# A hybrid-attention layer on one core: squares of the norms in two f32r parts, another booked clock, another plan, and the first low parts on VectorE

## The chip, the core and the metric

The kernel runs on one core of a Trainium2 chip. The metric is the device time of one execution in microseconds (us); a version's time is the median of several runs.

## What is computed

One layer on 528 tokens (16 meta tokens and 512 of the sequence) of width 1024, all in float32. The mixer has three kinds of attention with their own projections out of one matrix w_in: stick-breaking (sb, 4 heads), index-selected sparse attention (sp, 4 heads, the 132 best keys of each query by an index score), and differential attention (df, 4 heads, each the difference of two softmaxes). A gated sum of the three goes through w_out, then follows a convolutional gated feed-forward part. What the change touches are the norms of the heads:

```python
def _rmsnorm(a, gain):
    af = a.astype(jnp.float32)
    af = af * lax.rsqrt(jnp.mean(af * af, axis=-1, keepdims=True) + EPS)
    return (af * gain.astype(jnp.float32)).astype(a.dtype)
...
    q_df = _rmsnorm(q_df.reshape(b, tp, DF_HEADS, 2, HEAD_DIM), q_norm_df)
    k_df = _rmsnorm(k_df.reshape(b, tp, DF_HEADS, 2, HEAD_DIM), k_norm_df)
...
    y_df = _rmsnorm(y_df, subln_df) * (1.0 - lam_init)
```

q and k of sp are normed in the same way (over 64 elements); the output of df over 128.

## The kernel before, in words

**Precision.** A float32 product is made of three f32r products: every weight chunk (128 x 1024) and every activation is split into a high part (rounded to f32r by ScalarE) and a low part (the rest, by a subtraction), and mm3 (L336) runs high x high, high x low and low x high into one bank. A chunk used by the projections costs 48 matmuls, 24 for each half of the tokens.

**Chunks.** The 133 weight chunks are used in a fixed order (list order, made from the plan). prep (L315) loads one on SP's queue, rounds it on ScalarE and subtracts on VectorE or, through sub (L108), on VectorE or GpSimd, whichever the booked clock says is done first, VectorE with a handicap of 1000 ns. From the eleventh chunk on every second one (set two, L296) takes another way: two DMAs on GpSimd's queue with a negated copy on ScalarE between, so that no engine subtracts.

**The order of the work.** PLAN (L46) lists the stages. sb0, df2, sp1 and the like are units of two heads (df: one head of double width): q, k and v are projected by three chunks, and then generators take over: q_stream and k_stream (L665, L683) norm, split and move q and k by DMAs on SP's queue into the layout of the scores; v_stream (L701) transposes v; weight_stream (L880) makes the attention weights, one unit after another (after_unit, L1002), for sp only when the selection of the keys (topk_stream, L590) is done; value_stream (L893) multiplies by v; y_stream (L986) norms (df only) and splits the output. g0a and the like are four gate chunks each. b0a and the like are the branch products of one kind; branch (L1050) waits by until (L233) for the outputs of all units of its kind: b0 needs sb0 and sb1, b2 needs df0 to df3, b1 needs sp0 and sp1.

**The booked clock.** The program text is laid out by a planner in Python: mm, V, S and G add a cost to a clock of their engine (book, L77; Timed, L83; pe, L124), and each generator has a time at which its last result should be there (the engine's clock plus LAT). tick (L195), called after every eight matmuls, lets every generator go on; settle (L222) holds one back until TensorE's clock is past its results, ease (L228) until VectorE's clock is not far ahead of TensorE's. So the booked costs decide how early or late side work is put between the projections' matmuls. The queues themselves are in order, and buffers are counted: 13 tmp tiles, 12 qk tiles (a unit takes 6), 2 v, 8 y, 8 banks.

**headnorm** (L639) is the norm of q, k and the df outputs. It takes four tmp tiles: squares (ScalarE), then for each half of the tokens one float32 matmul with a constant matrix (blk: blocks of -0.5/64; ones2: -0.5/128) that sums over the head, then rstd (L428: logarithm, exponential and square on ScalarE) and rstd2 (L435: two operations on VectorE), at the end one multiplication on VectorE. It is called 16 times: for q and k of the two sp and four df units, and for the four df outputs. In the profile all matmuls are on L183, all operations of ScalarE, VectorE and GpSimd on L99.

Of the kernel before, what the change touches and what calls it, by code (L numbers as in the profile page):

```python
# [8 lines left out]
F32 = mybir.dt.float32  # L9
F32R = mybir.dt.float32r  # L10
AF = mybir.ActivationFunctionType
OP = mybir.AluOpType
# [3 lines left out]
P = 128  # L16
# [26 lines left out]

PLAN = "sb0 sb1 g0a df0 df1 g2a g0b df2 b0a b0b df3 g2b sp0 sp1 b2a b2b g1a g1b b1a b1b"  # L46
UNITS = {"sb": 0, "sp": 2, "df": 4}
BRW, BRO = (2, 2, 4), (0, 2, 4)

# [1 line left out]
def nk(i):  # L51
    return NM + P * (i + 1)
# [3 lines left out]
def tile_kernel(ctx: ExitStack, tc, hT, wpk, par, bias, yT):  # L56
    nc = tc.nc
# [5 lines left out]

    clock = {"P": 0.0, "V": 0.0, "S": 0.0, "G": 0.0}
    main = {"t": 0.0}
    cur = [main]
    LAT = 150.0
    SLACK = 1800
    BSL = 500
    PACE = 13000  # L70
# [6 lines left out]
    def book(e, cost):  # L77
        c = cur[0]
        clock[e] = max(clock[e], clock["P"]) + cost
        c["t"] = max(clock[e], c["t"] + cost, clock["P"] + cost) + LAT  # L80

    class Timed:
# [11 lines left out]
        def __getattr__(self, op):  # L94
            f = getattr(self.eng, op)

            def run(out, *a, **k):
# [2 lines left out]

            return run

    V = Timed("V", nc.vector, 1.04, 150, scalar_tensor_tensor=(1.25, 105), tensor_tensor_scan=(2.16, 110),
              tensor_tensor_reduce=(1.0, 255), match_replace=(1.04, 220))
    S = Timed("S", nc.scalar, 0.84, 190)
    G = Timed("G", nc.gpsimd, 2.3, 200)

    def sub(out, a, b, hv=HV):  # L108

# [14 lines left out]
    def pe(cost):  # L124
        c = cur[0]
        ready = c["t"] if c["t"] != c.get("pe") and c is not main else 0
        clock["P"] = max(clock["P"], ready) + cost
        c["t"] = c["pe"] = clock["P"] + LAT


    const = ctx.enter_context(tc.tile_pool(name="const", bufs=1))
# [44 lines left out]
    def tmp(dt=F32):  # L176
        return ap_.tile([P, T], dt, tag="tmp", bufs=caps["tmp"], name="tmp")

    def mm(out, lhsT, rhs, **k):

        n, w = rhs.shape[-1], 0.84 * max(32, lhsT.shape[-1])
        pe(max(0.46 * n + 1, w) if rhs.dtype == F32R else 2 * max(0.844 * n, w))
        PE.matmul(out, lhsT, rhs, **k)  # L183
# [38 lines left out]
    def settle(more=0):  # L222

        c = cur[0]
        while clock["P"] < c["t"] + more + SLACK:
            yield
# [23 lines left out]
    make_identity(nc, ident)  # L250
    onesd = const.tile([P, P], F32, name="onesd")
    V.memset(onesd, -0.5 / D)
    ones2 = const.tile([P, P], F32, name="ones2")
    V.memset(ones2, -0.5 / 128)
    blk = const.tile([P, P], F32, name="blk")
    V.memset(blk, 0.0)
    V.memset(blk[0:64, 0:64], -0.5 / 64)
    V.memset(blk[64:128, 64:128], -0.5 / 64)
    eps = const.tile([P, 1], F32, name="eps")
    V.memset(eps, EPS)  # L260
    one = const.tile([P, 1], F32, name="one")
# [15 lines left out]
    wraw, wsp = {}, {}  # L277
    plan = PLAN.split()
    order = [W_IX, W_QIX, W_QIX + 1]
    for w in plan:  # L280
# [5 lines left out]
        else:  # L286
            n = BRW[br] // 2
# [8 lines left out]
    two = set(order[10:order.index(W_OUT):2])  # L296
# [18 lines left out]
    def prep(k):  # L315
        if k is None or k in wsp:
            return
        assert k not in two
        load(k)
        r = wraw[k]  # L320
        wh, wl = parts_of(k)
        S.copy(wh, r)
        a = after.get(k)
        if a in two:
            V.tensor_tensor(wl, r, wh, OP.subtract)
        else:
            sub(wl, r, wh, HVW)
        load(a)
        if a in two:
            wh, wl = parts_of(a)  # L330
            gdma(wh, chunk(a))
            S.activation(wl, wh, AF.Copy, scale=-1.0)
            book("G", 1050)
            nc.gpsimd.dma_start(wl, chunk(a), accum_op=OP.add)  # L334
# [76 lines left out]
    ixd, st = [wbank(), wbank()], [wbank(), wbank()]  # L411
# [27 lines left out]
    y0, a0 = tmp(), tmp()  # L439
# [150 lines left out]
    def topk_stream():  # L590
        cur[0]["t"] += TKS
        yield from settle()
        for i in range(NB):
            c0 = 2 + P * i
            V.memset(work[i][:, nk(i):], -2e38)
            for j in range(8):
                for o, n in pieces(i):
                    yield from wait("tmp")
                    yield from ease(2000)
                    st, b = yield from bank("w")  # L600
                    cur[0]["t"] = 0
                    mm(st[:, :n], qst[j // 4][:, j % 4, c0:c0 + P], kst[:, o:o + n], start=True, stop=True)
                    r = tmp()
                    S.activation(r[:, :n], st[:, :n], AF.Relu)
                    drop(b)
                    x = r[:, :n]
                    acc = cmask[:, 384 - P * i + o:384 - P * i + o + n] if j == 0 else work[i][:, o:o + n]
                    if i == 0:
                        x = rev(x)
                        acc = acc if j else rev(acc)  # L610
                    V.scalar_tensor_tensor(work[i][:, o:o + n], x, wcol[:, i, j:j + 1], acc,
                                           OP.mult, OP.subtract if i == 0 and j == 0 else OP.add)
                    give("tmp")
        give("y")
        for r in range(-(-TOPK // 8)):
            t0 = clock["P"]
            for i in range(NB):
                left = count[i] - 8 * r
                if left <= 0:
                    continue  # L620
                yield from ease(500)
                m8 = ap_.tile([P, 8], F32, tag="m8", bufs=8, name="m8")
                book("V", 1.04 * nk(i) + 140)

                tc.keep_in_program_order(V.max(m8, work[i]))
                if left < 8:
                    V.memset(m8[:, left:], -2e38)
                V.match_replace(work[i], m8, work[i], -3e38)
                yield
            while clock["P"] < t0 + PACE:  # L630
                yield

        V.tensor_scalar(negs[0], rev(work[0][:, :nk(0)]), -3e38, NEG, OP.is_equal, OP.mult)
        for n in negs[1:]:
            V.tensor_scalar(n, n, -3e38, NEG, OP.not_equal, OP.mult)
        picked.append(1)


    def headnorm(raw, n, gain, mat):  # L639

        yield from wait("tmp", 4)
        sq, r, y0, a = tmp(), tmp(), tmp(), tmp()
        S.activation(sq[:, :n], raw[:, :n], AF.Square)
        yield from settle()
        for o, w in (HALQ if n == TQ else HALF):
            t0 = cur[0]["t"]
            st, b = yield from bank("w")
            cur[0]["t"] = 0
            mm(st[:, :w], mat, sq[:, o:o + w], start=True, stop=True)
            x = r[:, o:o + w], st[:, :w], y0[:, o:o + w], a[:, o:o + w]  # L650
            rstd(*x, now=False)
            yield from settle(-SET)
            rstd2(*x)
            drop(b)
            yield
        V.scalar_tensor_tensor(raw[:, :n], raw[:, :n], gain, r[:, :n], OP.mult, OP.mult)
        give("tmp", 4)
# [449 lines left out]
    for m in range(8):  # L1107
        nc.sync.dma_start(hm[:, m], hT[:, m, Q0:])
        k = W_OUT + m
# [19 lines left out]
        sq = ss if m == 0 else ft()  # L1129
# [36 lines left out]
    for f in range(NF):  # L1166
# [11 lines left out]
        a = ft()  # L1178
# [9 lines left out]
    for m in range(8):  # L1188
# [3 lines left out]
        for c in sorted({e // 8 for e in range(e0, e1)}):  # L1192
            k = W_DN + c
# [4 lines left out]
                start=es[0] == e0, stop=es[-1] == e1 - 1)  # L1198
# [77 lines left out]
```

## Time and profile before

| | us |
|---|---|
| median of 3 runs | 896.43 (896.34 to 900.48) |
| profiled execution | 900.03 |
| its span, first to last instruction | 898.2 |

| engine | busy us | share of the span |
|---|---|---|
| TensorE (PE) | 870.2 | 97% |
| VectorE (DVE) | 536.1 | 60% |
| ScalarE (ACT) | 454.6 | 51% |
| GpSimd (POOL) | 248.9 | 28% |

A row of a group of instructions reads: line, engine, operation, tile written <- tiles read, shape, x count | busy us, mean ns of one | idle time before them <- who ended it. A row of the timeline begins with start and duration in us; instructions of one group that follow each other are merged (x8), and the idle time of the engine before them stands in brackets with the releaser. A row of windows gives for a stretch the busy time of each engine, with the number of instructions begun, and PEclk, the granted share of TensorE's clock. A float32 matmul leaves two records in the trace, an f32r one a single record. The mixer's part ends near 474 us; then follow w_out and the feed-forward part.

### The profile page before, as it was taken

The page shows a single profiled execution, that of the slowest core. Times are in us where ns is not written, and L with a number is a line of the kernel's source. Part 1 is how long each engine was busy: PE and PEld are TensorE (multiplying, and loading weights), DVE is VectorE, ACT ScalarE, POOL GpSimd, SP SyncE. Part 2 cuts the span into 40 slices and gives each one's busy share as a digit, 9 for nine tenths or more (in the row PEclk, how much of TensorE's full clock was granted, in tenths as well). Part 3 has the DMA queues.
Part 4 walks back from the last instruction along what each step waited for, and adds up shares of the span by engine and source line. Part 5 has one row for each costly group of instructions (what it writes and reads, how often), then busy time and mean ns, then how long its engine had stood idle before and what let it go on. Part 6 is the DMA issues. An engine that isn't in the chain of part 4 may idle for free.

```text
span 898.2 us, 15407 instructions
## 1 busy us (share of the span) xinstructions
PE 870.2 (97%) x6066; PEld 807.8 (90%) x6066; DVE 536.1 (60%) x1145; ACT 454.6 (51%) x848; POOL 248.9 (28%) x200
## 2 busy tenths in 40 slices
PE   7899999999999999799999999999999999999998
PEld 6888999999998999699999999999999999888886
DVE  7669969888887787686457544444454544322221
ACT  7457887787756687645553443333333333211110
POOL 2334012122112111664034234444444444200100
PEclk9999999999999999899999999999999999999999
DMA  6666635574547645544454323233333322333330
GB/s 235 163 177 210 163 86 124 133 168 111 121 109 156 164 105 137 120 125 92 121 118 164 96 94 94 94 94 94 95 93 95 92 88 92 103 117 106 118 104 27
DMA packets 35959, 107.79 MB, mean 120 GB/s; under 512 B 4713, under 2 KB 4857, under 8 KB 35888
## 3 DMA queue, kind: packets, MB, share of 16 engines
q1 hardware_dynamic: 27968, 78.19, 28.7%
q0 software_dynamic: 7920, 28.64, 14.9%
q8 instruction: 47, 0.77, 0.4%
q14 instruction: 24, 0.20, 0.1%
HBM read 93.99 MB, written 5.86 MB: 111 GB/s over the span
## 4 chain that ended last, share of the span: by engine, by line
PE 72%; DVE 9%; ACT 7%; DMA 6%; issue 5%; POOL 1%; SPq 1%; ACTq 0%; POOLq 0%; DVEq 0%
PE psd L183 50%; PE psw L183 21%; DVE tmp L99 4%; ACT tmp L99 3%; DMA wl<-wpk 2%; DMA qk<-qk 2%; PE psw L187 2%; DVE work L99 1%; DMA wr<-wpk 1%; DVE wl L99 1%; DMA wh<-wpk 1%; DVE m L99 1%; ACT wl L99 1%; ACT G L99 1%; ACT wh L99 1%
## 5 line engine op out<-in xcount | busy, mean ns | idle before, releaser
L99 ACT CAST wh<-wr 128x1024 fp32r<-128x1024 f32 (+2 forms) x112 | 114.1, 1021 | 201.6 <-DMA wr<-wpk 168.5
L99 DVE TENSOR_TENSOR wl<-wr,wh 128x1024 fp32r<-128x1024 f32 (+2 forms) x80 | 96.2, 1203 | 71.6 <-PE psd L183 67.9
L99 POOL TENSOR_TENSOR wl<-wr,wh 128x1024 fp32r<-128x1024 f32 x32 | 81.5, 2548 | 176.6 <-PE psd L183 95.0
L183 PE MATMUL psd<-xh,wh 128*128 128x258 f32 (+2 forms) x792 | 118.9, 289 | 4.0 <-DVE tmp L99 3.5
L183 PE MATMUL psd<-xl,wh 128*128 128x258 f32 (+2 forms) x792 | 118.2, 289 | 0.0
L183 PE MATMUL psd<-xh,wl 128*128 128x258 f32 (+2 forms) x792 | 116.7, 288 | 1.2 <-POOL wl L99 1.1
L183 PEld LDWEIGHTS psd<-xh,wh 128*128 128x128 f32 x792 | 104.7, 190 | 5.7 <-issue 3.6
L183 PEld LDWEIGHTS psd<-xh,wl 128*128 128x128 f32 x792 | 104.1, 190 | 2.4 <-POOL wl L99 1.3
L183 PEld LDWEIGHTS psd<-xl,wh 128*128 128x128 f32 x792 | 104.4, 191 | 0.5
L99 ACT ACTIVATE tmp<-tmp 128x528 f32<-128x528 f32 (+7 forms) x154 | 69.6, 475 | 17.2 <-DVE tmp L99 14.6
L99 POOL TENSOR_TENSOR ft<-ft 128x512 f32<-128x512 f32 x22 | 47.1, 2140 | 83.5 <-DVE ft L99 83.5
L99 DVE SCALAR_TENSOR_TENSOR ft<-ft,prm 128x512 f32<-128x512 f32 x44 | 48.0, 1090 | 30.1 <-ACT ft L99 29.3
L334 POOL DMA_DIRECT2D wl<-wpk x25 | 22.2, 888 | 130.1 <-ACT wl L99 105.6
L183 PE MATMUL psw<-uh,wh 128*128 128x256 f32 (+2 forms) x264 | 47.0, 320 | 0.0
L183 PE MATMUL psd<-ul,wh 128*128 128x258 f32 (+2 forms) x264 | 46.9, 319 | 0.0
L183 PE MATMUL psw<-ul,wh 128*128 128x256 f32 (+2 forms) x264 | 46.9, 319 | 0.0
L183 PE MATMUL psd<-uh,wl 128*128 128x258 f32 (+2 forms) x264 | 46.8, 319 | 0.0
L183 PE MATMUL psw<-uh,wl 128*128 128x256 f32 (+2 forms) x264 | 46.8, 319 | 0.0
L183 PE MATMUL psd<-uh,wh 128*128 128x258 f32 (+2 forms) x264 | 46.8, 319 | 0.0
L183 PE MATMUL psd<-al,wh 128*128 128x512 f32 x176 | 45.8, 396 | 0.0
L183 PE MATMUL psd<-ah,wl 128*128 128x512 f32 x176 | 45.8, 396 | 0.0
L183 PE MATMUL psd<-ah,wh 128*128 128x512 f32 x176 | 45.8, 396 | 0.0
(196 smaller groups left out, 1674.7 us busy)
## 6 DMA issues: line engine op xcount, KB each, us to landing
wr<-wpk SPq DMA_DIRECT2D x106, 512.0 KB, 3.6
wh<-wpk POOLq DMA_DIRECT2D x25, 512.0 KB, 3.9
wl<-wpk POOLq DMA_DIRECT2D x25, 512.0 KB, 5.6
qk<-qk SPq DMA_DIRECT2D x48, 132.0 KB, 2.5
gd<-tab SPq DMA_DIRECT2D x8, 328.0 KB, 5.5
tmp<-hT SPq DMA_DIRECT2D x8, 264.0 KB, 6.2
W<-gd POOLq DMA_DIRECT2D x8, 264.0 KB, 3.9
qk<-tmp SPq DMA_DIRECT2D x16, 128.5 KB, 4.4
```

The costliest lines, as they stand in the source:

```text
L99: return f(out, *a, **k)
L183: PE.matmul(out, lhsT, rhs, **k)
L187: PE.transpose(out, x, ident[:x.shape[0], :x.shape[0]])
L334: nc.gpsimd.dma_start(wl, chunk(a), accum_op=OP.add)
```

## The change

The norms' squares are written twice by ScalarE, once in float32 and once rounded to f32r, VectorE makes their difference, and two f32r matmuls take the place of a float32 one; blk and ones2 become f32r (their values are exact in it), and the later tiles r and a reuse the squares' tile. The low part of a chunk among the first eleven goes to VectorE whatever the clock says. In the plan df2 and g0b change places, and sp0 and g2b. The booked costs of VectorE, ScalarE and GpSimd lose 60 to 100 ns of fixed cost each, and LAT, the time from the end of an operation to the next engine's start, rises from 150 to 250 ns.

```diff
-PLAN = "sb0 sb1 g0a df0 df1 g2a g0b df2 b0a b0b df3 g2b sp0 sp1 b2a b2b g1a g1b b1a b1b"
+PLAN = "sb0 sb1 g0a df0 df1 g2a df2 g0b b0a b0b df3 sp0 g2b sp1 b2a b2b g1a g1b b1a b1b"
...
-    LAT = 150.0
+    LAT = 250.0
...
-    V = Timed("V", nc.vector, 1.04, 150, scalar_tensor_tensor=(1.25, 105), tensor_tensor_scan=(2.16, 110),
-              tensor_tensor_reduce=(1.0, 255), match_replace=(1.04, 220))
-    S = Timed("S", nc.scalar, 0.84, 190)
-    G = Timed("G", nc.gpsimd, 2.3, 200)
+    V = Timed("V", nc.vector, 1.04, 70, scalar_tensor_tensor=(1.25, 30), tensor_tensor_scan=(2.16, 40),
+              tensor_tensor_reduce=(1.0, 180), match_replace=(1.04, 140))
+    S = Timed("S", nc.scalar, 0.84, 90)
+    G = Timed("G", nc.gpsimd, 2.3, 140)
...
-    ones2 = const.tile([P, P], F32, name="ones2")
-    V.memset(ones2, -0.5 / 128)
+    ones2 = const.tile([P, P], F32R, name="ones2")
+    V.memset(ones2.bitcast(F32), -0.5 / 128)
...
         a = after.get(k)
-        if a in two:
+        if a in two or k in order[:11]:
             V.tensor_tensor(wl, r, wh, OP.subtract)
         else:
             sub(wl, r, wh, HVW)
...
-                book("V", 1.04 * nk(i) + 140)
+                book("V", 1.04 * nk(i))
...
         yield from wait("tmp", 4)
-        sq, r, y0, a = tmp(), tmp(), tmp(), tmp()
+        sq, sh, sl, y0 = tmp(), tmp(F32R), tmp(F32R), tmp()
         S.activation(sq[:, :n], raw[:, :n], AF.Square)
+        S.activation(sh[:, :n], raw[:, :n], AF.Square)
+        V.tensor_tensor(sl[:, :n], sq[:, :n], sh[:, :n], OP.subtract)
+        r, a = sq, sq
         yield from settle()
         for o, w in (HALQ if n == TQ else HALF):
             t0 = cur[0]["t"]
             st, b = yield from bank("w")
             cur[0]["t"] = 0
-            mm(st[:, :w], mat, sq[:, o:o + w], start=True, stop=True)
+            mm(st[:, :w], mat, sh[:, o:o + w], start=True, stop=False)
+            mm(st[:, :w], mat, sl[:, o:o + w], start=False, stop=True)
```

blk is changed as ones2 is.

## Rows read from the trace of the kernel before

**Rows 1.** The page, busy us (share of the span) and instructions of two engines.

```profile
PE 870.2 (97%) x6066; PEld 807.8 (90%) x6066; DVE 536.1 (60%) x1145; ACT 454.6 (51%) x848; POOL 248.9 (28%) x200
```

**Rows 2.** Windows: two stretches of the mixer, then the feed-forward part.

```profile
60.00:80.00 20.00, 17.30 (x137) 16.32 (x136) 19.97 (x46) 14.47 (x40) 12.43 (x7) 1.00 0.54 175
...
360.00:380.00 20.00, 14.50 (x82) 12.36 (x82) 12.67 (x42) 12.91 (x35) 11.83 (x12) 0.83 0.57 125
...
480.00:890.00 410.00, 410.00 (x2437) 362.31 (x2436) 173.46 (x218) 131.39 (x161) 114.32 (x53) 1.00 0.32 101
```

**Rows 3.** Windows: the stretches with a granted clock of 0.50.

```profile
32.50:35.90 3.40, 3.40 (x17) 3.17 (x16) 1.57 (x5) 0.83 (x3) 0.00 (x0) 0.50 0.81 292
...
281.70:285.10 3.40, 3.40 (x19) 3.31 (x18) 0.84 (x8) 1.66 (x8) 1.36 (x2) 0.50 0.95 220
...
370.40:377.20 6.80, 6.57 (x30) 6.02 (x28) 5.64 (x24) 3.42 (x12) 5.14 (x5) 0.50 0.24 56
```

**Rows 4.** Groups of the norms' matmuls, then the timeline of TensorE near 357 us.

```profile
L183 PE MATMUL psw<-tmp,blk 128*128 128x264 f32 (+2 forms) x48 | 14.6, 390 | 0.3 <-ACT tmp L99 0.2
L183 PE MATMUL psw<-tmp,ones 128*128 128x258 f32 (+1 forms) x16 | 4.8, 383 | 0.0
...
356.58 0.59 PE L183 MATMUL psw<-tmp,blk 128*128 128x256 f32 x2
...
357.99 1.14 PE L183 MATMUL psd<-xl,wh 128*128 128x264 f32 x8
...
358.97 1.13 PE L183 MATMUL psd<-xh,wl 128*128 128x264 f32 x8
```

**Rows 5.** Groups by form on ScalarE and VectorE, and one row of the timeline.

```profile
L99 ACT ACTIVATE tmp<-tmp 128x514 f32<-128x514 f32 x10 | 6.3, 627 | 0.0
L99 DVE TENSOR_TENSOR tmp<-tmp 128x528 f32<-128x528 f32 x11 | 9.7, 881 | 0.2
...
15.48 0.70 DVE L99 TENSOR_TENSOR tmp<-tmp 128x528 f32<-128x528 f32 x1
```

**Rows 6.** The timeline: low parts on GpSimd and what stands beside them.

```profile
20.44 4.76 POOL L99 TENSOR_TENSOR wl<-wr,wh 128x1024 fp32r<-128x1024 f32 x2 [15.83 <-DVE tmp L99]
...
27.81 2.35 POOL L99 TENSOR_TENSOR wl<-wr,wh 128x1024 fp32r<-128x1024 f32 x1 [2.60 <-PE psw L183]
...
28.32 2.12 DVE L99 TENSOR_TENSOR kst<-tmp 32x264 fp32r<-32x264 f32 x1
...
30.93 0.42 DVE L99 TENSOR_TENSOR kst<-tmp 32x264 fp32r<-32x264 f32 x1
...
31.05 1.20 PE L183 MATMUL psd<-xh,wh 128*128 128x258 f32 x8 [3.47 <-DVE tmp L99]
...
71.36 5.32 POOL L99 TENSOR_TENSOR wl<-wr,wh 128x1024 fp32r<-128x1024 f32 x1 [4.21 <-issue]
...
76.74 1.26 PE L183 MATMUL psd<-xh,wl 128*128 128x264 f32 x8 [1.10 <-POOL wl L99]
...
258.60 1.22 DVE L99 TENSOR_TENSOR wl<-wr,wh 128x1024 fp32r<-128x1024 f32 x1
```

**Rows 7.** The timeline: df2's q norm, and its first scores.

```profile
243.11 0.60 PE L183 MATMUL psw<-tmp,blk 128*128 128x258 f32 x2
...
260.62 0.65 PE L183 MATMUL psw<-tmp,blk 128*128 128x256 f32 x2
...
281.38 0.48 PE L183 MATMUL psw<-qk 128*2 128x16 f32 x3 [1.93 <-DMA qk<-qk]
```

**Rows 8.** The timeline: b2a's first products, and df3's output.

```profile
360.18 1.08 PE L183 MATMUL psd<-y,wh 128*128 128x258 f32 x6
...
370.96 0.62 ACT L99 CAST y<-tmp 128x514 fp32r<-128x514 f32 x1 [0.27 <-DVE tmp L99]
```

More of the change, by code (lines that the diff above doesn't have):

```diff
@@ L252, in tile_kernel @@
     V.memset(onesd, -0.5 / D)
-    ones2 = const.tile([P, P], F32, name="ones2")
-    V.memset(ones2, -0.5 / 128)
[L255 to L258, printed above, removed]
+    ones2 = const.tile([P, P], F32R, name="ones2")
+    V.memset(ones2.bitcast(F32), -0.5 / 128)
+    blk = const.tile([P, P], F32R, name="blk")
+    V.memset(blk.bitcast(F32), 0.0)
+    V.memset(blk.bitcast(F32)[0:64, 0:64], -0.5 / 64)
+    V.memset(blk.bitcast(F32)[64:128, 64:128], -0.5 / 64)
     eps = const.tile([P, 1], F32, name="eps")
```

## The prediction

> **What bounds the kernel now.** I read the page's busy times first, then the windows, then the timeline around the idle places of TensorE. TensorE is busy 870.2 us of the 898.2 us span and VectorE 536.1 us [rows 1], so the end is set by TensorE's queue: time is won where TensorE gets less work or waits less. From 480 us on (w_out's tail, the feed-forward part) TensorE is busy all of 410 us at the full clock [rows 2]; the diff touches nothing there. The change is decided in the first 480 us, where TensorE has holes. The reader is to see in the windows that two are deep: 60 to 80 us has 17.30 us of TensorE beside a VectorE that is busy 19.97 of 20, and 360 to 380 us has 14.50 [rows 2]. The third group shows what a hole costs behind itself: after each of the waits near 28, 280 and 366 us the granted clock is 0.50 (1.2 of the two levels 1.2 and 2.4 GHz) for 3.4, 3.4 and 6.8 us [rows 3]. At half the clock half of such a stretch is lost: 1.7, 1.7 and 3.4 us.
>
> **Part 1, the squares' products in f32r.** headnorm's matmul runs in float32 today: 48 records with blk and 16 with ones2, two for each matmul, so 32 matmuls (16 norms, two halves each) [rows 4]. One of them with the eight projections behind it lasts from 356.58 to 357.99, 1.41 us; the next eight alone 0.98 us, to 358.97 [rows 4]. So it takes 1.41 - 0.98 = 0.43 us of the queue. It becomes two f32r matmuls of the same width, which at 0.98 / 8 take 0.245 us. The record count stays as it is, 64. Gain 32 x 0.185 = **5.9 us**, all of it on TensorE's queue.
>
> Each norm gets a second Square on ScalarE, 0.63 us [rows 5], 10.1 us in all, and a subtraction on VectorE. The nearest rows for that: 0.70 us undisturbed, 0.88 us as the mean of eleven 528-column forms, some of which collided with GpSimd [rows 5]. I take 0.70, the same operation and operands when nothing else runs: 16 x 0.70 = 11.2 us, at most 14.1. Both lie beside projections' matmuls, which do not wait for a norm. But the norm's product now waits for VectorE as well as for ScalarE, and TensorE's queue is in order: what stands behind it are projections, scores and transposes, and settle's booked time is all that keeps it from being issued too early. The cover ends where a norm is late, as df3's output norm is in front of b2a. There 0.63 + 0.70 = 1.3 us is added to the wait. Together with a few waits at queue heads I put **+2 us** for it, between 0 (all covered) and +5 (a third of the 14.1 us uncovered). No buffer is added: r and a now overwrite the squares.
>
> **Part 2, the first chunks' low parts.** Chunks 3 to 9 of the order have their low part on GpSimd: seven subtractions, the first in the pair at 20.44 us, the last at 71.36 us [rows 6]. The rule k in order[:11] puts all seven on VectorE, 1.22 us each [rows 6], 8.5 us more for it. What goes: the row at 28.32 shows kst's subtraction taking 2.12 us while GpSimd's low part ran from 27.81 to 30.16; its twin at 30.93 took 0.42 [rows 6]. TensorE waited 3.47 us for an evacuation queued behind it (31.05 us) and 1.10 us at 76.74 us for a low part that needed 5.32 us on GpSimd [rows 6]. Against that, a low part of 1.22 us can now stand in VectorE's queue ahead of that same evacuation, and behind it the next operations of the stick-breaking and index scores. At 28 us I book 1.70 - 1.22 = 0.5 us won, at 76 us the 1.10 us, and half a microsecond for the rest: **-2 us**. Bounds: -6 (both waits and the half-clock stretch at 32.5 us gone) and +3 (two and a half low parts added where VectorE is full, at 60 to 80 us).
>
> The skill bears on this. The row shows a two-input VectorE subtraction that lasted until GpSimd's ended. The Trainium skill, page "SBUF — State Buffer", section "Who interferes with whom", says that a VectorE instruction with two SBUF inputs and a GpSimd instruction that reads SBUF lock each other out for the whole instruction. That speaks for part 2, but against part 1: the 16 new subtractions have that form. If every one met GpSimd as kst did, they would cost 16 x 1.70 = 27 us of VectorE on top; by that the last rival below would be likelier, while the sum by the rows stands.
>
> **Part 3, the plan.** df2 moves ahead of g0b, sp0 ahead of g2b; no instruction is added. Today df2's q norm has its first product at 243.11 us and its second at 260.62 us [rows 7]: b0a and b0b ran between, whose evacuations fill VectorE. Its scores then stop TensorE for 1.93 us at 281.38 us, for the DMA that moves q and k [rows 7], and the half clock follows. With four gate chunks behind df2 its norms run before b0a. I take the 1.9 + 1.7 us as won, less a little: **-3.5 us** (0 to -3.6). The larger hole is b2a: its first six products run at 360.18 us, and df3's output is rounded for them only at 370.96 us [rows 8]. That hole is 20 - 14.50 = 5.5 us idle plus 3.4 us of half clock, 8.9 us. df2's weights and values out of df3's way bring df3 forward, but df3 keeps its distance to b2a, and sp0's two norms now follow it directly in place of a gate. I take half, **-4.5 us**; bounds -8.9 (gone) and +8.9 (as long again).
>
> SP's queue gets the same moves of q and k in another order; GpSimd's queue loses seven subtractions, and the chunk loads it issues for every second chunk stay.
>
> **Part 4, the booked clock.** It issues nothing. Lower fixed costs and a larger latency change where ease and settle release work. The trace of before has no row for that; the nearest are the waits of 1 to 2 us above, of one or two more or fewer: **0**, between -3 and +4.
>
> **Sum.** -5.9 + 2 - 2 - 3.5 - 4.5 + 0 = -13.9 us. The profiled execution took 900.03 us (span 898.2 and 1.8 around it): 886.1. It stands 3.6 us above the median of 896.43, so the forecast for the median is 896.4 - 13.9 = **882.5 us**.
>
> **The rivals.** *The hole at b2a stays.* df3's place relative to b2a is unchanged, so its output may come just as late: then -9.4 us, 887. For it: the sum of the work between them is the same; against it: df2's late norm, which now goes ahead. Chance 0.20.
> *All holes close.* -5.9 - 5.5 - 3.6 - 8.9 = -24, 872.5 us. The lower booked cost of VectorE would have to release the norms early everywhere. Chance 0.07.
> *sp0's norms delay df3 (slower).* Its place is between df3 and b2a. Headnorm takes four of 13 tmp buffers, as do df3's weights; if df3's k norm, weights or output norm are held once as df2's q norm is today, 260.62 - 243.11 = 17.5 us, b2a's hole grows by that: -9.4 + 17.5 = +8, 904.5. It decides from the point at which df3's output comes over 9.4 us later relative to b2a's first product than the 10.8 us of today. Against it: g2b's chunks now lie behind sp0 and give time. Chance 0.13.
> *VectorE sets the pace.* 8.5 us of low parts and 11 to 14 us of subtractions, or more with collisions, go to an engine that is full at 60 to 80 us [rows 2]; TensorE's saved 5.9 us and the closed waits come back as waits for evacuations. -13.9 + 14 = 0, 896. Against it: 12.67 of 20 at the large hole [rows 2]. Chance 0.15.
>
> **How the numbers follow.** A measurement here can tell about 0.5% (4.5 us) from no change. The forecast, 878 to 888, has 0.45; the first two rivals, 0.27, are faster as well: faster 0.72, same 0.15 (VectorE), slower 0.13 (sp0). The range leaves out the slower rival and the lower end of the closed holes: 872 to 898, which also holds the bounds of the parts unless most of them fall to one side.
>
> **What would show it.** Right: blk and ones2 products at a pitch of an ordinary f32r matmul; 16 more VectorE and ScalarE operations on tmp; no low part on GpSimd before 100 us and kst at 0.42 us; df2's scores without a DMA wait and the clock at full behind them; TensorE over 16 of 20 us around b2a's start. Wrong: a new TensorE wait of several microseconds with a half clock behind it, above all at b2a or at the first use of sp0's or sp1's q and k; or VectorE over 19 of 20 us in window after window from 100 to 340 us.

## The result and the profile after

The changed kernel took 905.71 us (median of four runs, 903.97 to 909.14), the kernel before 896.38 us beside it: a ratio of 1.0103, 95% interval 1.0065 to 1.0142. It is slower by 1%, where 882.5 us was forecast. The profiled execution took 907.28 us, its span is 905.5 us. In after TensorE's matmuls are on L184 and its transposes on L188 (L183 and L187 before); L99 is as before.

The page of after, busy times of the engines:

```profile
PE 871.6 (96%) x6066; PEld 809.1 (89%) x6066; DVE 549.0 (61%) x1171; ACT 459.2 (51%) x864; POOL 227.5 (25%) x190
```

VectorE has 26 instructions and 12.9 us more than in [rows 1], GpSimd 21.4 us less, TensorE as many records as before. Of the 26, 16 are the new subtractions and seven the low parts; the other three come from the planner, which also picks by its booked clock whether VectorE or GpSimd makes the low part of q, k and the outputs. So the parts were built as described; the 7.3 us that the span grew is not work that was added to TensorE.

A trace shows one execution, and the executions of a version differ with the granted clock (of the changed kernel's four, 903.97 us had 0.992 over the whole span and the profiled one 0.985; e1's trace below is of its longest execution, 907.34 us, f1's of one near its shortest, 893.50 us), so a time read from a single trace can be some microseconds off, while a place in a queue is the same in each.

Windows of after (start:end and length, then busy us and instructions of PE, PEld, DVE, ACT, POOL, then the granted clock, DMA share, GB/s):

```profile
20.00:40.00 20.00, 20.00 (x161) 19.43 (x160) 12.86 (x32) 11.21 (x25) 1.49 (x1) 1.00 0.55 148
60.00:80.00 20.00, 15.56 (x125) 14.61 (x123) 17.76 (x45) 11.72 (x31) 3.87 (x3) 0.98 0.75 214
360.00:380.00 20.00, 17.06 (x117) 14.84 (x117) 17.16 (x42) 14.52 (x36) 7.32 (x7) 0.90 0.44 113
400.00:420.00 20.00, 16.43 (x137) 15.77 (x135) 13.70 (x35) 5.98 (x17) 13.58 (x14) 1.00 0.53 127
```

The reader is to see three things. At 20 to 40 us TensorE never stops. At 60 to 80 us it stops longer than in [rows 2], with a VectorE that is less full. At 360 to 380 us it is busier than in [rows 2], with 4.5 us more of VectorE, and a new hole stands at 400 to 420 us, where the window of before was full:

```profile
400.00:420.00 20.00, 20.00 (x170) 19.75 (x170) 14.64 (x54) 10.39 (x26) 9.76 (x10) 1.00 0.41 107
```

Windows of after, the stretches with a granted clock of 0.50 (0.51):

```profile
79.20:82.60 3.40, 3.07 (x14) 3.06 (x15) 1.38 (x6) 3.40 (x13) 0.93 (x1) 0.51 0.99 252
174.80:181.60 6.80, 6.65 (x32) 6.50 (x33) 2.38 (x12) 2.90 (x10) 0.00 (x0) 0.50 0.28 80
256.70:263.50 6.80, 5.37 (x27) 5.10 (x26) 1.74 (x5) 3.18 (x2) 0.00 (x0) 0.50 0.72 171
372.80:376.20 3.40, 3.40 (x16) 2.57 (x14) 2.57 (x10) 2.26 (x9) 0.14 (x1) 0.50 0.77 141
379.60:383.00 3.40, 3.40 (x18) 3.40 (x18) 3.22 (x8) 2.38 (x6) 0.00 (x0) 0.50 0.00 0
420.60:424.00 3.40, 3.40 (x20) 3.08 (x18) 3.33 (x11) 2.13 (x6) 0.00 (x0) 0.50 0.00 0
```

That is 27.2 us in six stretches, against 13.6 us in three in [rows 3]. The stretches at 32.5 and 281.7 us are gone; 79, 175, 257 and 421 us are new places. What stood ahead of them or in them is in the timeline of after (start, duration, the engine's idle time before in brackets), six rows of TensorE, one of ScalarE and one of SP's queue:

```profile
71.08 1.26 PE L184 MATMUL psd<-xh,wl 128*128 128x264 f32 x8 [0.92 <-DVE wl L99]
...
78.11 1.04 ACT L99 CAST wh<-wr 128x1024 fp32r<-128x1024 f32 x1 [3.23 <-DMA wr<-wpk]
...
79.53 0.81 PE L188 MATMUL psw<-ident,tmp 128*16 128x128 f32 x3 [3.13 <-ACT tmp L99]
...
165.65 7.60 SPq L666 DMA_DIRECT2D qk<-qk  x6
...
174.95 0.49 PE L184 MATMUL psw<-qk 128*2 128x16 f32 x2 [2.74 <-issue]
...
255.78 0.51 PE L184 MATMUL psd<-y,wl 128*128 128x258 f32 x2 [2.03 <-DMA wl<-wpk]
...
259.85 0.49 PE L184 MATMUL psw<-qk 128*2 128x16 f32 x2 [1.43 <-issue]
...
419.54 0.39 PE L184 MATMUL psw<-pm,vm 96*128 96x258 f32 x1 [3.01 <-DVE pm L99]
```

The causes differ: ScalarE's queue, held at 78.11 us by the rounding of a chunk that had come late; for df0's scores at 175 us and df2's at 260 us most likely the moves of q and k (the profile names no releaser, but ahead of 175 us SP's queue issues them until 173.25 us); a low part loaded by DMA at 255.78 us, ahead of the half clock at 256.7 us; VectorE. What they share is that the order of the queues is another: matched in longest common blocks, 4445 of the 6066 TensorE records of before stand in the old order.

The hole at b2a, first TensorE, then VectorE and ScalarE, in the timeline of after:

```profile
368.85 0.88 PE L184 MATMUL psd<-y,wh 128*128 128x258 f32 x6
...
372.22 0.40 PE L184 MATMUL psw<-tmp,ones 128*128 128x258 f32 x2
...
375.64 0.72 PE L184 MATMUL psw<-tmp,ones 128*128 128x256 f32 x2
...
381.29 0.75 DVE L99 SCALAR_TENSOR_TENSOR tmp<-tmp,gsub 128x514 f32<-128x514 f32 x1
...
383.13 0.62 ACT L99 CAST y<-tmp 128x514 fp32r<-128x514 f32 x1
```

df3's output is rounded 14.3 us behind b2a's first products, against 10.8 us in [rows 8], and 12.2 us later than there in absolute time. TensorE is less idle meanwhile because sp0's weights (pm, pt, transposes) now run there; VectorE does their evacuations ahead of the multiplication by gsub.

### The profile page after: what moved, and what is told of

The parts are those of the page before. It is cut to its first block, busy times and chain, and to the rows that moved or that the text cites. A ratio compares the mean times of both kernels' runs of the same rounds, so it can differ in the third digit from the quotient of the medians.

```text
span 905.5 us, 15435 instructions
## 1 busy us (share of the span) xinstructions
PE 871.6 (96%) x6066; PEld 809.1 (89%) x6066; DVE 549.0 (61%) x1171; ACT 459.2 (51%) x864; POOL 227.5 (25%) x190
## 4 chain that ended last, share of the span: by engine, by line
PE 80%; DVE 9%; ACT 4%; issue 3%; DMA 2%; POOL 1%; SPq 0%; DVEq 0%; ACTq 0%; POOLq 0%
PE psd L184 56%; PE psw L184 23%; DVE tmp L99 4%; ACT tmp L99 2%; PE psw L188 2%; DMA wr<-wpk 1%; DVE work L99 1%; DVE wl L99 1%; DVE m L99 1%; ACT G L99 1%; DMA qk<-tmp 1%; DVE G L99 1%; POOL G L99 1%; DVE pm L99 0%; ACT wl L99 0%
## 5 line engine op out<-in xcount | busy, mean ns | idle before, releaser
L99 ACT CAST wh<-wr 128x1024 fp32r<-128x1024 f32 (+2 forms) x112 | 114.0, 1019 | 206.6 <-DMA wr<-wpk 165.5
L99 DVE TENSOR_TENSOR wl<-wr,wh 128x1024 fp32r<-128x1024 f32 (+2 forms) x87 | 103.7, 1193 | 74.2 <-PE psd L184 57.4
L184 PE MATMUL psd<-xh,wh 128*128 128x258 f32 (+2 forms) x792 | 119.7, 288 | 1.6 <-ACT wh L99 1.1
L184 PE MATMUL psd<-xl,wh 128*128 128x258 f32 (+2 forms) x792 | 118.6, 288 | 0.0
L184 PE MATMUL psd<-xh,wl 128*128 128x258 f32 (+2 forms) x792 | 117.0, 286 | 0.9 <-DVE wl L99 0.9
L184 PEld LDWEIGHTS psd<-xh,wh 128*128 128x128 f32 x792 | 105.1, 191 | 2.4 <-ACT wh L99 1.4
L184 PEld LDWEIGHTS psd<-xl,wh 128*128 128x128 f32 x792 | 105.4, 192 | 0.1
L184 PEld LDWEIGHTS psd<-xh,wl 128*128 128x128 f32 x792 | 104.1, 190 | 1.3 <-DVE wl L99 1.1
L99 POOL TENSOR_TENSOR wl<-wr,wh 128x1024 fp32r<-128x1024 f32 x25 | 60.7, 2426 | 132.6 <-ACT wh L99 59.1
L99 ACT ACTIVATE tmp<-tmp 128x528 f32<-128x528 f32 (+9 forms) x170 | 77.7, 489 | 9.6 <-DVE tmp L99 8.2
L99 POOL TENSOR_TENSOR ft<-ft 128x512 f32<-128x512 f32 x22 | 47.1, 2142 | 83.5 <-DVE ft L99 83.5
L99 DVE SCALAR_TENSOR_TENSOR ft<-ft,prm 128x512 f32<-128x512 f32 x44 | 51.8, 1177 | 25.4 <-ACT ft L99 24.6
L184 PE MATMUL psw<-uh,wh 128*128 128x256 f32 (+2 forms) x264 | 47.0, 320 | 0.0
L184 PE MATMUL psd<-ul,wh 128*128 128x258 f32 (+2 forms) x264 | 46.9, 319 | 0.0
L184 PE MATMUL psw<-ul,wh 128*128 128x256 f32 (+2 forms) x264 | 46.9, 319 | 0.0
L184 PE MATMUL psd<-uh,wl 128*128 128x258 f32 (+2 forms) x264 | 46.8, 319 | 0.0
L184 PE MATMUL psw<-uh,wl 128*128 128x256 f32 (+2 forms) x264 | 46.8, 319 | 0.0
L184 PE MATMUL psd<-uh,wh 128*128 128x258 f32 (+2 forms) x264 | 46.8, 319 | 0.0
L184 PE MATMUL psd<-al,wh 128*128 128x512 f32 x176 | 45.8, 396 | 0.0
L184 PE MATMUL psd<-ah,wl 128*128 128x512 f32 x176 | 45.8, 396 | 0.0
L184 PE MATMUL psd<-ah,wh 128*128 128x512 f32 x176 | 45.8, 396 | 0.0
```

The costliest lines, as they stand in the source:

```text
L99: return f(out, *a, **k)
```

## The experiments

18 kernels, each timed in 6 to 12 runs against the kernel before on the same chip, whose median was 896.9 to 900.5 us there. The chip is not the same for all of them, so kernels are compared by their ratios and not by their times. "y" is the time at which the profile shows df3's output being rounded: 370.96 in the kernel before, 383.13 after. Ratios have their 95% interval.

### Each part alone

e1_norm: headnorm and the two constants as in the diff above. e2_lows, e3_plan, e4_book:

```diff
-        if a in two:
+        if a in two or k in order[:11]:          # e2_lows
...
-PLAN = "... g2a g0b df2 b0a b0b df3 g2b sp0 sp1 b2a ..."
+PLAN = "... g2a df2 g0b b0a b0b df3 sp0 g2b sp1 b2a ..."          # e3_plan
...
-    LAT = 150.0
+    LAT = 250.0          # e4_book, with V, S, G and the 140 as in the change
```

> The kernel before with the norms' part alone (float32 product replaced by two f32r ones, second Square, subtraction). By the term of the prediction: 32 x 0.185 = 5.9 us less TensorE, 2 us of waits more, so 892 against 896. If the norm's new wait for VectorE or its longer chain (1.3 us) eats the saving, 896 and more, and the norms' products show waits for VectorE. If any edit only reshuffles the layout, anything between 891 and 901 with the waits at other places than before.

> The kernel before with the first chunks' low parts on VectorE alone. If the 3.5 us by which the first projection starts earlier in the changed kernel are kept: 892 to 894. If the chunk loads set the pace of the first 90 us (the changed kernel waits 3.3 us at 76 us behind a late load): the start comes 3.5 us earlier, the 60 to 80 us stretch gives it back, 896.

> The kernel before with the new plan alone. Theory 'plan': sp0 in front of g2b puts sp0's norms and weights in the way of df3's output, which then comes 90 us or more after df3's last projection; the hole at b2a stays at 10 us or grows: 900 to 906. Theory 'booked clock': the plan is innocent or helps (df2's wait at 281 us gone): 888 to 896.

> The kernel before with the booked costs and LAT alone. Theory 'booked clock': side work is issued too early, TensorE waits at the heads of its queue (first scores of a unit for the q and k DMAs, transposes behind a blocked ScalarE) in four or more places with the half clock behind them: 901 to 908. Theory 'plan': 894 to 898, no new waits over 2 us.

| kernel | us | ratio | y, us |
|---|---|---|---|
| e1_norm | 902.08 | 1.0062 (1.0035 to 1.0089) | 379.2 |
| e2_lows | 901.73 | 1.0037 (1.0016 to 1.0058) | 373.5 |
| e3_plan | 902.89 | 1.0054 (1.0022 to 1.0085) | 374.7 |
| e4_book | 901.60 | 1.0052 (1.0030 to 1.0073) | 357.4 |

All four are slower, by 0.4 to 0.6%, though e4 neither adds nor removes work (four subtractions go from GpSimd to VectorE) and e3 only moves it. They don't add up to the change either: the four sum to 2.05%, the change costs 1.03%. e2, which came out above both of its expectations, is the clearest: its df3 is projected 11.5 us earlier than before (267.9 against 279.4 us), and its output comes 2.6 us later. What the four have in common is that each lays the queues anew. y alone doesn't order the kernels: e4's output comes 13.6 us earlier than before, and e4 is slower all the same.

### The order held, and the order alone

f1 and f2 make the new instructions but book what the old ones cost, so that the planner makes nearly the same decisions: matched as above, 6056 of the 6066 TensorE records keep the old order in f1, 6030 in f2 (in e1: 5075); the expectations count the places of 6017 instructions. n1 and n3 add and remove no instruction and change only the planner's margin SLACK, in ns. The pieces without a remark are f1 against e1.

```diff
-        S.activation(sh[:, :n], raw[:, :n], AF.Square)
-        V.tensor_tensor(sl[:, :n], sq[:, :n], sh[:, :n], OP.subtract)
+        nc.scalar.activation(sh[:, :n], raw[:, :n], AF.Square)
+        nc.vector.tensor_tensor(sl[:, :n], sq[:, :n], sh[:, :n], OP.subtract)
...
-            mm(st[:, :w], mat, sh[:, o:o + w], start=True, stop=False)
-            mm(st[:, :w], mat, sl[:, o:o + w], start=False, stop=True)
+            pe(2 * max(0.844 * w, 0.84 * P))
+            PE.matmul(st[:, :w], mat, sh[:, o:o + w], start=True, stop=False)
+            PE.matmul(st[:, :w], mat, sl[:, o:o + w], start=False, stop=True)
...
+        elif k in order[:11]:          # f2 alone
+            t = clock["P"]
+            onG = max(clock["G"], t) + G.cost(wl) < max(clock["V"], t) + V.cost(wl) + HVW
+            book("G" if onG else "V", (G if onG else V).cost(wl))
+            nc.vector.tensor_tensor(wl, r, wh, OP.subtract)
...
-    SLACK = 1800
+    SLACK = 1900          # n1_slack; 1700 in n3_slack_less
```

> The norms' part alone, booked as the kernel before books it (the two f32r products at the float32 product's price, the second Square and the subtraction not booked), so that the order of the queues stays: 6008 of TensorE's 6017 places as before. Theory 'own cost': the part itself is slow (a longer chain, more VectorE), so it stays at 901 to 903 as with its own booking. Theory 'layout': the part is worth its 5.9 us of TensorE less at most 2 us of waits, 891 to 893, and the 5 us by which the part alone was slower came from the queues' new order.

> The norms' part and the low parts on VectorE, both booked as before, 5983 of 6017 places of TensorE kept. Theory 'own cost': 901 or more. Theory 'layout': the low parts bring 2 to 3.5 us more than the norms alone, 888 to 891; if the hole at b2a swallows an earlier start (it did where the low parts ran with their own booking), the same as the norms alone, 891 to 893.

> The kernel before with one planner constant moved by 100 ns (SLACK 1900 for 1800). No instruction is added or taken away, 4468 of TensorE's 6017 places stay as they were. Theory 'layout': the order of before is a good one among many, and a new order of itself costs 2 to 8 us: 899 to 905. Theory 'own cost': 895 to 898.

> As the run before, the other way (SLACK 1700), 5086 of 6017 places kept. Theory 'layout': 899 to 905. Theory 'own cost': 895 to 898. If one of the two comes out faster than 894, the order of before is no special one and the parts' losses need another cause.

| kernel | us | ratio | y, us |
|---|---|---|---|
| f1_norm_same_layout | 895.77 | 0.9985 (0.9957 to 1.0014) | 365.2 |
| f2_both_same_layout | 894.93 | 0.9978 (0.9956 to 1.0001) | 365.1 |
| n1_slack | 912.75 | 1.0185 (1.0147 to 1.0223) | 388.1 |
| n3_slack_less | 895.53 | 0.9985 (0.9955 to 1.0015) | 361.1 |

A margin larger by 100 ns, with no instruction added (two subtractions go from GpSimd to VectorE), costs more than the whole change; one smaller by 100 ns costs nothing, where 899 to 905 us were expected if every new order loses. The window of n1_slack over b2a:

```profile
360.00:380.00 20.00, 15.17 (x64) 11.19 (x64) 17.06 (x50) 13.86 (x42) 8.32 (x9) 0.66 0.18 42
380.00:400.00 20.00, 13.10 (x80) 11.35 (x80) 13.26 (x37) 9.25 (x27) 8.14 (x9) 0.83 0.18 41
```

64 and 80 matmuls begin there, where the full window of after, 20 to 40 us, has 161. And the norms, slower by 0.6% in e1, are not slower at all with the order held. The timeline of e1_norm, df3's first scores and its output:

```profile
319.83 0.77 PE L183 MATMUL psw<-qk 128*2 128x16 f32 x6
...
379.21 0.62 ACT L99 CAST y<-tmp 128x514 fp32r<-128x514 f32 x1 [2.94 <-DVE tmp L99]
```

The same two places in f1_norm_same_layout:

```profile
301.21 0.48 PE L183 MATMUL psw<-qk 128*2 128x16 f32 x4
...
365.22 0.62 ACT L99 CAST y<-tmp 128x514 fp32r<-128x514 f32 x1 [0.27 <-DVE tmp L99]
```

Counted in TensorE's records, 2298 stand ahead of df3's first scores in f1, as in the kernel before, and 2394 in e1: 96 places further back, only because the new operations were booked.

### Parts of the changed kernel undone, and the plan on the held kernel

a1 and e6 start from the changed kernel, p1 and p4 from f2.

```diff
-    SLACK = 1800
+    SLACK = 1700          # a1_after_slack_less
...
-PLAN = "... g2a df2 g0b b0a b0b df3 sp0 g2b sp1 b2a ..."
+PLAN = "... g2a g0b df2 b0a b0b df3 g2b sp0 sp1 b2a ..."          # e6_no_plan
...
-PLAN = "... g2a g0b df2 b0a b0b df3 g2b sp0 sp1 b2a ..."
+PLAN = "... g2a df2 df3 g0b b0a b0b g2b sp0 sp1 b2a ..."          # p1_df3_early
+PLAN = "... g2a df2 g0b df3 b0a b0b g2b sp0 sp1 b2a ..."          # p4_df3_mid
```

> The changed kernel with SLACK 1700 for 1800, nothing else: another order of the same work. Theory 'layout': its 905.7 us is one draw of many, and this one lies anywhere from 893 to 913, by over 4 us from 905.7 as likely as not; the time follows df3's output (383 us in the changed kernel). Theory 'change itself' (the plan or the booked clock costs its 9 us in any order): 903 to 908.

> The changed kernel with the plan of before. Theory 'plan' (sp0 in front of g2b delays df3's output): df3's output comes before 370 us, 895 to 900. Theory 'booked clock': 901 to 908, with waits at first scores as in the changed kernel at 172 and 259 us. Theory 'layout': anything, following df3's output.

> The norms' and the low parts booked as before (894.9 us so far), with a plan in which df2 and df3 both stand ahead of g0b, b0a and b0b: 46 us more of TensorE's work lie between df3's projections and b2a. If b2a waits for df3's output because that is too near behind its projections, the output comes 20 us or more ahead of b2a, its hole (7 us idle and 10 us of half clock) goes and the time is 884 to 889. If VectorE and the 13 tmp tiles are the limit, df3's output comes at 355 to 365 us as before and the time is 893 to 900; two units in a row may add waits at 200 to 260 us.

> As the run before, with df2 ahead of g0b and df3 ahead of b0a: 13 us more between df3 and b2a. By the distance: df3's output 5 to 13 us earlier relative to b2a, hole half gone, 888 to 892. If VectorE and the tmp tiles are the limit: 893 to 900.

| kernel | us | ratio | y, us |
|---|---|---|---|
| a1_after_slack_less | 907.17 | 1.0099 (1.0060 to 1.0138) | 384.4 |
| e6_no_plan | 903.06 | 1.0049 (1.0024 to 1.0075) | 366.6 |
| p1_df3_early | 895.11 | 0.9968 (0.9945 to 0.9991) | 363.1 |
| p4_df3_mid | 902.95 | 1.0053 (1.0024 to 1.0081) | 368.0 |

a1 speaks against mere chance: the changed kernel stays where it is in yet another order. e6, with the plan of before, has the time that was expected if the booked clock does the harm (901 to 908 us) and the early y that was expected if the plan does (before 370 us); its interval still meets the changed kernel's. p1 refutes a reading of b2a's hole: df3's projections end 40.2 us earlier than in f2 (235.6 against 275.8 us), and yet its scores begin at 300.0 us (301.3 in f2) and its output comes at 363.1, 2 us earlier. The distance between df3 and b2a in the plan is not what makes it late; what it waits for in place of that (the weights are made one unit after another) was not tried by itself.

### Booking or plan

p5, p2 and p6 put the plan's moves on f2, with the old booking and the new work unbooked. e5 and q1 are the changed kernel but for one thing each: e5 books with the old costs and LAT, q1 books the new work as the old (the lines of f1 and f2; in e5 and the changed kernel the two f32r products are also booked cheaper than the float32 one). e7 has sp0 back behind g2b.

```diff
+PLAN = "... g2a g0b df2 b0a b0b df3 sp0 g2b sp1 b2a ..."          # p5_sp0_early, from f2
+PLAN = "... g2a df2 g0b b0a b0b df3 g2b sp0 sp1 b2a ..."          # p2_df2_early, from f2; e7_plan_df2, from the changed kernel
+PLAN = "... g2a df2 g0b b0a b0b df3 sp0 g2b sp1 b2a ..."          # p6_plan_on_f2
...
-    LAT = 250.0
+    LAT = 150.0          # e5_no_book, with V, S, G and the 140 of before
```

> Norms and low parts held in the old order (895 us), booking of before, and of the plan only sp0 ahead of g2b. If sp0 ahead of g2b is what makes df3's output late in the changed kernel (383.1 us there, 365.1 with the order held), the output comes at 373 us or later, b2a lasts over 17 us and the time is 899 to 904 us. If the place of sp0 is harmless and the booked clock does the harm, the output stays within 3 us of 365 and the time within 2 us of 895.

> Norms and low parts held in the old order, booking of before, and of the plan only df2 ahead of g0b. If moving df2 forward is worth the 3.5 us of the prediction, the wait for the scores of df2 is gone and the time is 891 to 893 us. If it only brings the wait to another place, as the changed kernel's wait at 256 us suggests, 895 to 898 us.

> The changed kernel with the booked costs and the latency of before: norms, low parts and plan remain. If the booked clock is the larger part of the loss, 896 to 900 us, with the waits near 76, 173 and 256 us gone. If the plan is, 903 to 907 us, df3's output at 378 us or later.

> The changed kernel with sp0 back behind g2b: of the plan only df2 ahead of g0b remains, the booked clock is the new one. If sp0's place costs what lies between the changed kernel and the one with the old plan (905.7 against 903.1), this gives 902 to 903.5 us with df3's output at 370 us or earlier. If df2's move is the harm, it stays at 905 to 907 us.

> Norms and low parts without being booked (as in f2), the booking of before, and the whole new plan: against e5 only the booked cost of the new instructions differs. If the two moves of the plan are good in themselves and it is the booking of the new instructions, with the order that comes out of it, that costs, 891 to 894 us with df3's output before 365 us. If the two moves do harm together, 900 to 905 us, near e5's 904.8.

> The changed kernel with all its parts and its new booked costs, but the new squares, subtractions and products of the norms and the moved low parts are booked as the old ones were. If booking the new instructions is the harm, 893 to 898 us. If the new booked clock does as much by itself, 902 to 907 us, with df3's output at 375 us or later or with waits near 76 and 173 us as in the changed kernel.

| kernel | us | ratio | y, us |
|---|---|---|---|
| p5_sp0_early | 893.09 | 0.9946 (0.9925 to 0.9968) | 360.4 |
| p2_df2_early | 895.26 | 0.9969 (0.9948 to 0.9991) | 365.1 |
| e5_no_book | 904.79 | 1.0089 (1.0057 to 1.0122) | 380.6 |
| e7_plan_df2 | 908.90 | 1.0127 (1.0085 to 1.0169) | 374.1 |
| p6_plan_on_f2 | 898.09 | 0.9981 (0.9959 to 1.0003) | 369.5 |
| q1_after_unbooked | 899.24 | 1.0000 (0.9970 to 1.0029) | 368.5 |

The ladder reads: norms and low parts with the order held (f2) 0.9978; with the new plan (p6) 0.9981; with the new booked clock too (q1) 1.0000; and with the new work booked (the changed kernel) 1.0103. In their times p6 and q1 fell between their two expectations; by the ratio they stand at the kernel before. Three pairs differ in nothing but whether new work is booked: f1 and e1 (the norms alone), p6 and e5, q1 and the changed kernel. Booking costs 0.8, 1.1 and 1.0%, in each pair with intervals that don't meet. What it changes in the program is the order of the queues and the engine of a few subtractions (and with them a table load or two of ScalarE): one goes from GpSimd to VectorE in e1 and in e5; in the changed kernel three go there against q1 and one comes back. The other runs agree: the six kernels that book the new norms have 1.0049 to 1.0127, the eight that have them unbooked 0.9946 to 1.0053. It is not the distance from the old order: of the 6066 records q1 keeps 4404 in it, the changed kernel 4445. The changed kernel, df3's first scores (2354 records ahead of them on TensorE):

```profile
321.33 0.48 PE L184 MATMUL psw<-qk 128*2 128x16 f32 x4
```

q1_after_unbooked (2312 ahead), and its output:

```profile
314.61 0.17 PE L183 MATMUL psw<-qk 128*2 128x16 f32 x1
...
368.49 0.62 ACT L99 CAST y<-tmp 128x514 fp32r<-128x514 f32 x1 [0.39 <-DVE tmp L99]
```

Its window at b2a:

```profile
360.00:380.00 20.00, 19.13 (x162) 18.66 (x161) 16.02 (x37) 15.66 (x35) 6.30 (x6) 1.00 0.42 97
```

The same operations, the same plan, the same booked clock otherwise: 42 places in TensorE's queue, an output 14.6 us earlier, and no half clock at 360 to 380 us. In q1 b2a's first product runs at 373.12 us, when the output is there. Not every new wait of the changed kernel goes with the booking: q1 has the one near 175 us too, and the half clock behind it.

```profile
160.00:180.00 20.00, 16.74 (x123) 15.80 (x123) 17.54 (x43) 12.27 (x28) 5.61 (x6) 0.89 0.56 140
```

In p6 and e5 it is 118 places (2332 and 2450) and 11.1 us. e5_no_book's window at b2a:

```profile
360.00:380.00 20.00, 13.19 (x62) 10.63 (x61) 18.90 (x56) 13.59 (x43) 10.03 (x10) 0.67 0.32 75
```

The booked clock by itself is 1.0000 against 0.9981 (q1, p6) and 1.0103 against 1.0089 (the changed kernel, e5): no difference that these runs can tell, in this setting; alone, in e4, it cost 0.5%.

p5 beats both kernels: the norms and low parts unbooked, and sp0 ahead of g2b, 0.5% faster than before. Its output, then its window at b2a:

```profile
360.41 0.62 ACT L99 CAST y<-tmp 128x514 fp32r<-128x514 f32 x1 [0.38 <-DVE tmp L99]
```

```profile
360.00:380.00 20.00, 18.85 (x131) 17.76 (x131) 19.02 (x49) 8.87 (x25) 14.57 (x13) 0.83 0.42 109
```

With both moves (p6) this gain is lost again, and df2's move alone (p2) leaves f2 as it was. Against f2 (0.9956 to 1.0001) p5's interval overlaps, so that sp0's move itself gains is likely and not shown. e7 came out above both of its expectations: with the new work booked, taking sp0's move back gains nothing.

## Why the prediction was wrong

**The step that failed** stands between two sentences of part 1 and part 4. The text said that settle's booked time is what holds a norm's product back, and that part 4 "issues nothing"; it costed the booked constants at 0 and put no term at all for what booking 16 Squares, 16 subtractions and seven low parts does to the order. Every term was a duration in the order of before. The runs show that this missing term is the largest: +1.0% of 898 us, some 9 us (q1 to the changed kernel), with +0.8 and +1.1% in the other two pairs. The second step that failed is the size of part 3, -8 us, of which the moves brought nothing (p6 against f2). In steps of the ladder, forecast and measured: parts 1 and 2, -0.66% and -0.22%; part 3, -0.89% and +0.03%; part 4, 0 and +0.19% (within the noise); booking the new work, no term and +1.03%. Together that is -1.55% and +1.03%. Each measured step is a difference of two ratios that are known to 0.2 to 0.4% either way. The bounds of -3 to +4 us for part 4 were taken from single waits of 1 to 2 us; re-laying the queues moves several such waits and the half clock behind them at once, and n1_slack shows +1.85% from a margin alone.

How a longer booked chain becomes a later output is partly shown and partly argued. Shown: df3's scores stand 42 to 118 places further back, and its output comes 11 to 15 us later in the traces. Argued: by the constants of the planner, LAT included, a second Square and a subtraction on 528 columns add 0.78 + 0.85 = 1.6 us to what settle waits for, per norm. Measured, the two take 0.64 and 0.80 us. df3's first scores lie behind two norms of its own unit, q's and k's. An estimate of 2 x 1.6 = 3.2 us of TensorE's queue, at 0.12 us a matmul, is some 27 places: fewer than in any of the three pairs. The norms of the units before it can add to that, since the weights are made one unit after another, but no run holds this apart. Why the planner's other decisions fall as they do is open; a1, whose margin is smaller, did not repair it.

**Part 1, right in its durations, not in what they are worth.** Groups of after, the norms' products and the new operations by form:

```profile
L184 PE MATMUL psw<-tmp,blk 128*128 128x264 f32 (+2 forms) x48 | 11.7, 316 | 0.1
L184 PE MATMUL psw<-tmp,ones 128*128 128x258 f32 (+1 forms) x16 | 3.6, 310 | 0.0
...
L99 ACT ACTIVATE tmp<-tmp 128x514 fp32r<-128x514 f32 x10 | 6.2, 619 | 0.0
L99 ACT ACTIVATE tmp<-tmp 128x528 fp32r<-128x528 f32 x6 | 3.8, 637 | 0.0
...
L99 DVE TENSOR_TENSOR tmp<-tmp 128x514 fp32r<-128x514 f32 x10 | 8.2, 822 | 1.4 <-ACT tmp L99 0.9 <-DMA qk<-tmp 0.4
...
L99 DVE TENSOR_TENSOR tmp<-tmp 128x528 fp32r<-128x528 f32 x6 | 4.8, 800 | 0.3 <-ACT tmp L99 0.2
```

The timeline of after, the two halves of df2's q norm and the first product behind its eight projections, then new subtractions on VectorE beside GpSimd (the last is df3's output norm):

```profile
216.40 0.46 PE L184 MATMUL psw<-tmp,blk 128*128 128x258 f32 x2
...
221.85 0.41 PE L184 MATMUL psw<-tmp,blk 128*128 128x256 f32 x2
...
223.07 0.28 PE L184 MATMUL psw<-pm,vm 96*128 96x258 f32 x1
...
295.58 1.64 POOL L99 TENSOR_TENSOR tmp<-tmp,qk 128x514 fp32r<-128x514 f32 x1
296.48 1.32 DVE L99 TENSOR_TENSOR tmp<-tmp 128x528 fp32r<-128x528 f32 x1
...
355.30 1.04 POOL L99 TENSOR_TENSOR tmp<-W,work 128x400 f32<-128x400 f32 x1
355.51 1.39 DVE L99 TENSOR_TENSOR tmp<-tmp 128x514 fp32r<-128x514 f32 x1 [0.46 <-ACT tmp L99]
...
368.86 2.83 POOL L99 TENSOR_TENSOR tmp<-W,work 128x400 f32<-128x400 f32 x2
369.20 1.32 DVE L99 TENSOR_TENSOR tmp<-tmp 128x514 fp32r<-128x514 f32 x1
```

The record count stayed 64, a pair lasts 0.41 to 0.46 us where it lasted 0.59 to 0.65 [rows 4, 7]. With the eight projections behind it, it lasts from 221.85 to 223.07, 1.22 us in place of 1.41, so the saving on TensorE's queue is the forecast one. The Squares take 6.2 + 3.8 = 10.0 us (10.1 forecast), the subtractions 8.2 + 4.8 = 13.0 us (11.2 forecast, 14.1 at most). The net gain of 3.9 us is 0.43%; with the order held 0.15% was measured (f1), with an interval whose end, 0.9957, is at the forecast and whose other end, 1.0014, leaves no gain at all. df3's output comes 5.7 us earlier in f1's trace, the span is 6.5 us shorter (891.7 against 898.2 us); how much of that is the execution is open.

The 1.8 us above the forecast are three collisions. Thirteen of the sixteen took 0.68 to 0.71 us, as forecast; those at 296.48, 355.51 and 369.20 us took 1.32, 1.39 and 1.32 us, each beside an operation of GpSimd with two inputs in SBUF. One that ran beside a memset of GpSimd, at 212.19 us, took 0.69 us. That agrees with the Trainium skill, page "SBUF — State Buffer", section "Who interferes with whom": a VectorE instruction with two SBUF inputs contends with a GpSimd instruction that reads SBUF, and not with one that only writes it. The 27 us that the prediction worked out for every one colliding did not come: three met, at some 0.65 us each.

**Part 2, right where it was looked for, covered elsewhere.** VectorE in the timeline of after, kst's two subtractions:

```profile
26.08 0.42 DVE L99 TENSOR_TENSOR kst<-tmp 32x264 fp32r<-32x264 f32 x1
...
27.26 0.42 DVE L99 TENSOR_TENSOR kst<-tmp 32x264 fp32r<-32x264 f32 x1 [0.32 <-ACT tmp L99]
```

Both take 0.42 us, where the first took 2.12 [rows 6], and 20 to 40 us is full. The 1.10 us wait for GpSimd's low part at 76.74 us is gone, but 0.92 us for VectorE's at 71.08 and 3.13 us for ScalarE at 79.53 stand in its place. With the order held it is the same place that gives the gain back; the window of f1, then of f2:

```profile
60.00:80.00 20.00, 17.27 (x138) 16.29 (x137) 19.97 (x51) 12.76 (x35) 12.85 (x7) 1.00 0.61 202
...
60.00:80.00 20.00, 16.10 (x109) 15.24 (x109) 18.11 (x44) 10.49 (x29) 6.88 (x4) 0.83 0.82 250
```

f2 against f1 (0.9978, 0.9985) is a gain of 0.07%, too small to be told from none; 2 us, 0.22%, were forecast.

**Part 3, half right.** df2's q norm has its halves 221.85 - 216.40 = 5.5 us apart in place of 17.5, as forecast, and its first scores come 19.4 us earlier, at 259.85 us. In the kernel before, the row in [rows 7] is not the first: one record stands ahead of it.

```profile
279.27 0.17 PE L183 MATMUL psw<-qk 128*2 128x16 f32 x1
```

But they still wait, 1.43 us. A half clock is there too, now 6.8 us; it begins at 256.7 us, behind the wait for a low part at 255.78 us, and df2's wait lies inside it. So one wait went, and two others came. The hole at b2a was not halved. On the held kernel the two moves together are worth nothing (0.9981 against 0.9978) where 8 us were forecast.

**The rivals.** The slower one gave 904.5 us, and 905.7 was measured, but not by its mechanism: it was to decide from 9.4 us of added distance between b2a's first product and df3's output, and there are 3.5 (14.3 - 10.8). p5 shows that sp0 ahead of g2b does no harm in the held order. That VectorE sets the pace is not borne out either: it is busy 17.76 us at 60 to 80 us, where it was 19.97 [rows 2], and of the twelve windows from 100 to 340 us one is over 19 (19.81, at 140 to 160 us). So the time agreed with a rival's by coincidence, and none of them had the mechanism. The range, 872 to 898 us, and the 0.13 for slower were built from durations alone.

## What to carry to other kernels

Where the order of the queues is computed from booked costs, a change has two effects: what its instructions cost, and the order that their booking produces. Hold the order to measure the first (issue the new work without booking it), change a margin alone to see how large the second can be, and don't call an edit good or bad before both are known. In a profile the second shows as waits with unrelated causes at places where none were, and as the same instruction standing many places further back in a queue.

## What the runs showed of the hardware

A wait is dear by what follows it: in the changed kernel 6.8 us at a granted clock of 0.50 lie behind a wait of 2.74 us (at 174.95 us), and in n1_slack the granted clock over 40 us of the hole at b2a was 0.66 and 0.83. A float32 product of the norms, with eight f32r projections behind it, took 1.41 us of TensorE's queue, two f32r products of the same width 1.22 us; both leave two records. A VectorE subtraction of 514 or 528 columns with two inputs in SBUF took 0.68 to 0.71 us alone, and 1.32 to 1.39 us where it met a GpSimd operation that reads SBUF: three of sixteen did, with GpSimd busy 25% of the span.
